# VectorE adds the epsilon of the roots, and six products take their remainder terms last

## Chip, cores and metric

The kernel runs on one core of one Trainium2 chip. The metric is device time in microseconds (us): the median of three runs.

## The reference

Two layers on a sequence of 256 positions with model width 1024, in float32. Layer 0 mixes with block-sparse attention (16 heads of 64; with one block of 256 it is plain causal attention), layer 1 with differential attention (8 heads, two softmaxes each, and a root mean square norm per head). Each mixer is followed by a squared-ReLU MLP of width 4096. Both are modulated by a conditioning vector and closed with a layer norm:

```python
for i in range(DEPTH):
    shift1, scale1, gate1, shift2, scale2, gate2 = split(mod[i], 6)
    h = x * (1.0 + scale1) + shift1
    y = moba_attention(h, ...) if i % 2 == 0 else diff_attention(h, ...)
    x = layer_norm(DEEPNORM_ALPHA * x + (1.0 + gate1) * y, ln_g[i, 0], ln_b[i, 0])
    h = x * (1.0 + scale2) + shift2
    y = square(relu(h @ mlp_w_up[i])) @ mlp_w_down[i]
    x = layer_norm(DEEPNORM_ALPHA * x + (1.0 + gate2) * y, ln_g[i, 1], ln_b[i, 1])
```

`layer_norm` and the norm per head both need `rsqrt(variance + 1e-5)`.

## The kernel before

The 256 positions are two blocks of 128 (b = 0, 1). TensorE works on pairs of numbers: each operand is split into a rounded part (hi) and the remainder (lo). A product takes three terms per depth of 128: hi x hi, hi x lo of the weights, lo of the activations x hi (lines 165 to 169). Weights arrive by DMA on SP's queue into `raw`; ScalarE casts a piece of 128x1024 to `hi` (line 130), VectorE subtracts to get `lo` (line 131, "the split"). `hi` and `lo` have eight slots each; a piece covers two depths, a weight set of 512 columns has four pieces.

A string of steps, PROGRAM, gives the order in which work is traced. For layer 1 it begins `V00 Q00 T00 S0 V10 Q10 ...` (values, queries with keys, transposes, scores; first digit the block), the MLP begins `U00 U01 X00 U10 U11 X01 ... D00` (up, transpose, down), `B` and `C` close a sub-layer, and `f` fills in a row of the modulation's matrix-vector product (line 216, VectorE). Each engine runs its own queue in order. The queue's order is laid out by a planner when the program is built: by the order of tracing among what it then expects to be ready, with `tc.high_priority()` for some instructions (only the scores use it). So instructions of later steps can stand between two dependent ones.

A closing (`close`, `layer_norm`, `modulate`) runs per block, eight times: six inner ones and two at the end of the kernel. VectorE makes z from the product, the gate and the residual (lines 289, 292) and takes statistics (302, 303). `rsqrt_eps` has GpSimd add the epsilon (277) and raise to the power -0.5 (278). VectorE scales the first half of z (308), ScalarE the second (311). TensorE transposes z (320), ScalarE modulates it (324) and casts it to the rounded operand `hT` (327), VectorE takes the remainder (328). Then the products of the next step can begin: V (layer 1) or U. The attention of layer 1 calls `rsqrt_eps` once for each of its eight pairs of heads and block, between ScalarE's squares (465) and VectorE's scaling (468). In the last closing VectorE subtracts the mean beside GpSimd's root (598) and then scales (601).

Of the kernel before, what the change touches and what calls it, by code (L numbers as in the profile page):

```python
# [19 lines left out]
ALU = mybir.AluOpType  # L20
# [12 lines left out]
EPS = 1e-5  # L33
# [39 lines left out]
def tile_trunk(ctx: ExitStack, tc: tile.TileContext, x, c, moba_w_in, moba_w_out, diff_w_in, diff_w_out,  # L73
               lam_q1, lam_k1, lam_q2, lam_k2, subln_g, ada_wt, ada_b, ln_g, ln_b, w_up, w_down, cst, out):
    nc = tc.nc
    vec, act, pe, pool_e, sp = nc.vector, nc.scalar, nc.tensor, nc.gpsimd, nc.sync
# [10 lines left out]
    def psum(tag):  # L87
        return psp.tile([P, 512], F32, tag=tag, name=tag, bufs=NB[tag])
# [48 lines left out]
    def load_cols(w, segs):  # L137

        ops = []
        for r in range(2):  # L140
            raw = raw_tile()
            r3 = raw.rearrange("p (k n) -> p k n", n=512)
            o = 0
            for c0, n in segs:
                sp.dma_start(out=r3[:, :, o:o + n],
                             in_=w[r * 512:(r + 1) * 512, c0:c0 + n].rearrange("(k p) n -> p k n", p=P))
                o += n
            for q in range(2):
                hi, lo = split_piece(raw[:, q * 1024:(q + 1) * 1024])
                for k in range(2):  # L150
                    ops.append((hi[:, k * 512:(k + 1) * 512], lo[:, k * 512:(k + 1) * 512]))
        return ops
# [12 lines left out]
    def mm3(dst, lhs, rhs, start, stop):  # L165
        (xh, xl), (wh, wl) = lhs, rhs
        pe.matmul(dst, lhsT=xh, rhs=wh, start=start, stop=False)  # L167
        pe.matmul(dst, lhsT=xh, rhs=wl, start=False, stop=False)  # L168
        pe.matmul(dst, lhsT=xl, rhs=wh, start=False, stop=stop)  # L169

    def dense(dst, lhs, rhs):
        n = len(lhs)
        for k in range(n):
            mm3(dst, lhs[k], rhs[k], k == 0, k == n - 1)

    def dense2(dsts, lhs, rows, start, stop):

# [80 lines left out]
    def halves(t, b):  # L258

        return t[:, :, b * P:(b + 1) * P], t[:, :, (2 + b) * P:(3 + b) * P]  # L260

    def as_ops(pairs):
        return [(h[:, k, :], l[:, k, :]) for h, l in pairs for k in range(4)]

    def block_ops(tiles, b):
        return as_ops([halves(t, b) for t in tiles])
# [7 lines left out]
        return t  # L274

    def rsqrt_eps(dst, src):
        pool_e.tensor_scalar(out=dst, in0=src, scalar1=EPS, scalar2=None, op0=ALU.add)
        pool_e.tensor_tensor(out=dst, in0=dst, in1=nhalf.to_broadcast(list(src.shape)), op=ALU.pow)

    def layer_norm(b, accs, gate, parts=None):  # L280
# [59 lines left out]
    def v_cols(g2):  # L340
        return [(2 * D + g2 * 512, 512)]
# [227 lines left out]
        queue_vector(*key)  # L569


    def unit(w, hT):
        ps = psum("mm")
        dense(ps, hT, w)
        return ps

    def out_proj(dsts, g2, b, rows):
# [36 lines left out]
    def step_load(st, key, loader):  # L614
        if key not in st:
            st[key] = loader()
        return st[key]

    def step_v(st, b, g2):
        l = st["l"]  # L620
        if l == 0 and g2 == 0:
            ps = kacc[b][0]
        else:
            w = step_load(st, ("wv", l, g2), lambda: load_cols(w_ins[l], v_cols(g2)))
            ps = unit(w, block_ops(st["x"], b))
        evict_v(b, g2, ps)

    def step_qk(st, b, g):
# [25 lines left out]
    def step_up(st, b, j):  # L654
        l = st["l"]
        w = step_load(st, ("wu", l, j), lambda: load_cols(w_up[l], [(j * 512, 512)]))
        ps = psum("mm")
        dense(ps, block_ops(st["x"], b), w)
        r = ap_.tile([P, 512], F32, tag="nat", name="nat", bufs=3)
        act.activation(out=r, in_=ps, func=AF.Relu)  # L660
        act.activation(out=r, in_=r, func=AF.Square)
        st["r", b, j] = r
# [75 lines left out]
    st = {"x": hT0}  # L738
# [48 lines left out]
```

## Time and profile before

| what | before |
|---|---|
| median of three runs | 643.16 us (641.18 to 646.57) |
| profiled execution | 644.11 us, of which the span of its instructions 640.7 |
| granted TensorE clock | 0.997 of full speed |
| busy: TensorE, VectorE, ScalarE, GpSimd | 609.0, 500.4, 377.6, 22.2 us |

The span runs from the first to the last instruction of the trace. Rows name the line, the engine (PE is TensorE, PEld its weight loads, DVE VectorE, ACT ScalarE, POOL GpSimd), the operation and its tiles, output before input.

### The profile page before, as it was taken

How to read it: one execution, taken by the hardware profiler on the slowest of the kernel's cores; microseconds unless marked ns; L12 is line 12 of the kernel's file. 1: busy time of each engine (PE TensorE's matmuls, PEld its weight loads, DVE VectorE, ACT ScalarE, POOL GpSimd, SP SyncE). 2: the span in 40 equal slices, each digit the busy share in tenths (PEclk: the TensorE clock that was granted, in tenths of full speed). 3: DMA queues.
4: the chain of work that ended last, by engine and by line, in shares of the span. 5: the costliest groups of instructions: out<-in, count | busy, mean ns of one | idle time of the engine just before them, and what ended most of it. 6: DMA issues, size and time to landing. Idle time of an engine off the chain costs nothing.

```text
span 640.7 us, 8768 instructions
## 1 busy us (share of the span) xinstructions
PE 609.0 (95%) x3140; PEld 499.6 (78%) x3140; DVE 500.4 (78%) x903; ACT 377.6 (59%) x699; POOL 22.2 (3%) x37
## 2 busy tenths in 40 slices
PE   4889999998999999999999999989999999999994
PEld 3667887886888888888877787767788888888883
DVE  5798998889978878888799989977984646465446
ACT  3448665657846545664477676765775556475530
POOL 0000000001000000000000010021100000000002
PEclk9999999999999999999999999999999999999998
DMA  8997998876689888989765967682663764746401
GB/s 292 406 322 279 313 325 286 288 250 227 215 309 343 308 313 330 326 294 338 268 231 188 337 229 263 232 289 68 208 218 109 259 225 143 255 133 213 182 0 66
DMA packets 65941, 158.23 MB, mean 247 GB/s; under 512 B 4041, under 2 KB 21098, under 8 KB 65898
## 3 DMA queue, kind: packets, MB, share of 16 engines
q1 hardware_dynamic: 65898, 157.68, 70.1%
q8 instruction: 24, 0.39, 0.2%
q14 instruction: 19, 0.16, 0.1%
HBM read 156.62 MB, written 1.05 MB: 246 GB/s over the span
## 4 chain that ended last, share of the span: by engine, by line
PE 64%; DVE 18%; DMA 6%; ACT 4%; issue 3%; POOL 2%; SPq 1%; DVEq 0%; POOLq 0%; ACTq 0%
PE ac L184 13%; PE sc L184 10%; PE mm L687 7%; PE tp L687 6%; DMA aw<-in_ada_w_dram 6%; DVE lo L131 5%; DVE aw L216 4%; PE mm L167 4%; PE mm L169 4%; PE mm L168 4%; PE mm L692 3%; PE tp L692 3%; ACT hi L130 2%; DVE z L292 1%; DVE z L289 1%
## 5 line engine op out<-in xcount | busy, mean ns | idle before, releaser
L131 DVE TENSOR_TENSOR lo<-raw,hi 128x1024 fp32r<-128x1024 f32 x196 | 232.0, 1197 | 44.1 <-ACT hi L130 40.4
L130 ACT CAST hi<-raw 128x1024 fp32r<-128x1024 f32 x196 | 201.3, 1034 | 62.5 <-PE sc L184 43.6
L216 DVE CUSTOM_DVE_ANT_0 aw<-aw,sbc,tabT 128x1024 f32<-128x1024 f32 x96 | 122.0, 1280 | 23.1 <-DMA aw<-in_ada_w_dram 22.7
L167 PE MATMUL mm<-hi,hT 128*128 128x512 f32 x224 | 90.6, 405 | 6.1 <-ACT hi L130 3.2
L169 PE MATMUL mm<-hi,hT 128*128 128x512 f32 x224 | 89.0, 398 | 0.0
L168 PE MATMUL mm<-lo,hT 128*128 128x512 f32 x224 | 88.6, 396 | 0.2 <-DVE lo L131 0.2
L687 PE MATMUL mm<-hT,hi 128*128 128x512 f32 x192 | 60.4, 396 | 0.0
L687 PE MATMUL tp<-hT,hi 128*128 128x512 f32 x192 | 60.3, 395 | 0.0
L167 PEld LDWEIGHTS mm<-hi,hT 128*128 128x128 f32 x224 | 42.3, 189 | 16.1 <-ACT hi L130 3.8
L184 PE MATMUL ac<-hi,sTh 128*128 128x512 f32 x160 | 51.2, 397 | 0.0
L184 PE MATMUL ac<-lo,sTh 128*128 128x512 f32 x160 | 50.8, 394 | 0.0
L184 PE MATMUL ac<-hi,sTl 128*128 128x512 f32 x160 | 50.4, 392 | 0.0
L169 PEld LDWEIGHTS mm<-hi,hT 128*128 128x128 f32 x224 | 42.3, 189 | 9.1 <-DVE hT L328 0.4
L168 PEld LDWEIGHTS mm<-lo,hT 128*128 128x128 f32 x224 | 42.3, 189 | 8.6 <-DVE lo L131 0.3
L184 PE MATMUL sc<-hi,sTh 128*128 128x512 f32 x144 | 45.3, 392 | 0.0
L184 PE MATMUL sc<-lo,sTh 128*128 128x512 f32 x144 | 45.1, 391 | 0.0
L184 PE MATMUL sc<-hi,sTl 128*128 128x512 f32 x144 | 44.6, 390 | 0.0
L692 PEld LDWEIGHTS tp<-hT,lo 128*128 128x128 f32 x192 | 34.4, 188 | 7.5
L692 PEld LDWEIGHTS mm<-hT,lo 128*128 128x128 f32 x192 | 34.4, 188 | 7.3
L697 ACT COPY nat<-mm 128x256 f32<-128x256 f32 x24 | 7.8, 376 | 52.4 <-PE mm L687 52.4
L692 PE MATMUL tp<-hT,lo 128*128 128x256 f32 x192 | 36.0, 279 | 0.0
L692 PE MATMUL mm<-hT,lo 128*128 128x256 f32 x192 | 35.9, 279 | 0.0
(153 smaller groups left out, 899.4 us busy)
## 6 DMA issues: line engine op xcount, KB each, us to landing
aw<-in_ada_w_dram SPq DMA_DIRECT2D x96, 512.0 KB, 5.5
raw<-in_mlp_w_up_dram SPq DMA_DIRECT2D x32, 1024.0 KB, 5.9
raw<-in_mlp_w_down_dram SPq DMA_DIRECT2D x32, 1024.0 KB, 5.1
raw<-in_diff_w_in_dram SPq DMA_DIRECT2D x16, 512.0 KB, 5.1
raw<-in_moba_w_in_dram SPq DMA_DIRECT2D x24, 256.0 KB, 5.5
raw<-in_moba_w_in_dram SPq DMA_DIRECT2D x8, 512.0 KB, 4.8
raw<-in_moba_w_out_dram SPq DMA_DIRECT2D x4, 1024.0 KB, 8.4
raw<-in_diff_w_in_dram SPq DMA_DIRECT2D x4, 1024.0 KB, 5.7
```

Source lines behind the costliest of these rows:

```text
L130: act.copy(out=hi[:, :n], in_=raw_ap)
L131: vec.tensor_tensor(out=lo[:, :n], in0=raw_ap, in1=hi[:, :n], op=ALU.subtract)
L167: pe.matmul(dst, lhsT=xh, rhs=wh, start=start, stop=False)
L168: pe.matmul(dst, lhsT=xh, rhs=wl, start=False, stop=False)
L169: pe.matmul(dst, lhsT=xl, rhs=wh, start=False, stop=stop)
L184: pe.matmul(dsts[h], lhsT=a, rhs=w[:, h * 512:(h + 1) * 512], start=start and k == 0 and i == 0, stop=stop and k == n - 1 and i == 2)
L216: vec.tensor_tensor_reduce(out=aw, in0=aw, in1=sbc, scale=1.0, scalar=adab_cols(l, v)[:, j:j + 1], op0=ALU.mult, op1=ALU.add, accum_out=dst)
L289: vec.tensor_tensor(out=z[:, c_], in0=accs[c_.start // 512][:, a0:a0 + c_.stop - c_.start], in1=gate[:, c_], op=ALU.mult)
L292: vec.scalar_tensor_tensor(out=z[:, c_], in0=xt[b][:, c_], scalar=ALPHA, in1=z[:, c_], op0=ALU.mult, op1=ALU.add)
L687: pe.matmul(ps, lhsT=w[k][0][:, c_], rhs=x3[k], start=first, stop=last)
L692: pe.matmul(ps[:, 0:S], lhsT=w[k][1][:, c_], rhs=x3[k][:, 0:S], start=False, stop=False)
L697: act.copy(out=r[:, i * S:(i + 1) * S], in_=ps[:, S:2 * S])
```

## The change

VectorE adds the epsilon instead of GpSimd; the power stays on GpSimd. A product marked `late` runs its two terms with the rounded activations over all eight depths first, and then the eight terms with the remainder of the activations. Marked are V00 and V10 of layer 1 (in layer 0 the products with g2 = 0 are made elsewhere) and U00, U10 of both layers. Neither edit raises the priority of an instruction.

```diff
-    def dense(dst, lhs, rhs):
+    def dense(dst, lhs, rhs, late=False):
+
         n = len(lhs)
+        if not late:
+            for k in range(n):
+                mm3(dst, lhs[k], rhs[k], k == 0, k == n - 1)
+            return
         for k in range(n):
-            mm3(dst, lhs[k], rhs[k], k == 0, k == n - 1)
+            for i in range(2):
+                pe.matmul(dst, lhsT=lhs[k][0], rhs=rhs[k][i], start=k == 0 and i == 0, stop=False)
+        for k in range(n):
+            pe.matmul(dst, lhsT=lhs[k][1], rhs=rhs[k][0], start=False, stop=k == n - 1)
...
     def rsqrt_eps(dst, src):
-        pool_e.tensor_scalar(out=dst, in0=src, scalar1=EPS, scalar2=None, op0=ALU.add)
+        vec.tensor_scalar(out=dst, in0=src, scalar1=EPS, scalar2=None, op0=ALU.add)
         pool_e.tensor_tensor(out=dst, in0=dst, in1=nhalf.to_broadcast(list(src.shape)), op=ALU.pow)
...
-    def unit(w, hT):
+    def unit(w, hT, late=False):
         ps = psum("mm")
-        dense(ps, hT, w)
+        dense(ps, hT, w, late)
         return ps
...
-            ps = unit(w, block_ops(st["x"], b))
+            ps = unit(w, block_ops(st["x"], b), late=g2 == 0)
         evict_v(b, g2, ps)
...
-        dense(ps, block_ops(st["x"], b), w)
+        dense(ps, block_ops(st["x"], b), w, late=j == 0)
```

## Rows read from the trace of the kernel before

**Rows 1.** Busy time by stretch (from:to, length, then busy us per engine, clock, DMA).
```profile
135.00:175.00 40.00, 37.45 (x177) 29.97 (x176) 38.06 (x52) 30.32 (x48) 3.30 (x4) 1.00 0.63 215
175.00:318.00 143.00, 143.00 (x728) 121.47 (x726) 116.48 (x162) 78.25 (x113) 0.00 (x0) 1.00 0.89 316
318.00:350.00 32.00, 31.06 (x152) 24.68 (x151) 30.34 (x45) 23.57 (x40) 3.15 (x4) 1.00 0.60 199
350.00:437.00 87.00, 83.40 (x468) 65.54 (x469) 76.91 (x218) 59.15 (x163) 7.96 (x14) 1.00 0.75 266
437.00:476.00 39.00, 38.09 (x181) 30.63 (x180) 34.12 (x47) 29.67 (x51) 4.25 (x6) 1.00 0.44 140
...
620.00:640.70 20.70, 11.83 (x57) 9.59 (x55) 14.18 (x26) 1.07 (x2) 3.26 (x4) 0.90 0.13 51
sum 640.70, PE 608.99 PEld 499.60 DVE 500.36 ACT 377.60 POOL 22.21; mean PE 76.12 PEld 62.45 DVE 62.55 ACT 47.20 POOL 2.78
```

**Rows 2.** The chain that ended last, one of its pieces (start, us, what).
```profile
190.74 5.45 PE sc L184 x24
```

**Rows 3.** Waits: who waited for whom (us in total, times, longest).
```profile
DVE on L468 <- POOL ss L278: 6.4, 7, 1.6
PE tp L320 <- DVE nm L310: 1.8, 3, 1.0
PE tp L320 <- DVE z L308: 1.5, 3, 0.5
PE mm L167 <- ACT hT L327: 1.1, 1, 1.1
PEld mm L169 <- DVE hT L328: 0.4, 1, 0.4
```

**Rows 4.** Line 277 alone (ns min/median/max, first and last start, shapes).
```profile
L277 POOL TENSOR_SCALAR rs<-bna x8: 705/1044/1087, 142.8 to 634.5; 128x1 f32<-128x1 f32 x8
L277 POOL TENSOR_SCALAR ss<-ss x8: 217/266/1192, 368.0 to 437.6; 128x2 f32<-128x2 f32 x8
```

**Rows 5.** Timeline of the sixth closing, VectorE and GpSimd (start, us, what, idle before).
```profile
455.46 0.68 DVE L302 BATCH_NORM_STATS2 bns<-z 128x6 f32<-128x512 f32 x1
...
456.05 1.21 DVE L131 TENSOR_TENSOR lo<-raw,hi 128x1024 fp32r<-128x1024 f32 x1
...
457.17 0.20 DVE L303 BATCH_NORM_AGGREGATE bna<-bns 128x2 f32<-128x12 f32 x1
457.29 1.17 DVE L131 TENSOR_TENSOR lo<-raw,hi 128x1024 fp32r<-128x1024 f32 x1
...
457.47 1.08 POOL L277 TENSOR_SCALAR rs<-bna 128x1 f32<-128x1 f32 x1 [11.32 <-DVE bna L303]
...
458.63 0.58 POOL L278 TENSOR_TENSOR rs<-rs,nhalf 128x1 f32<-128x1 f32 x1
...
459.25 0.55 DVE L308 TENSOR_SCALAR z<-z,bna,rs 128x512 f32<-128x512 f32 x1 [0.78 <-POOL rs L278]
...
459.78 1.22 DVE L131 TENSOR_TENSOR lo<-raw,hi 128x1024 fp32r<-128x1024 f32 x1
```

**Rows 6.** Groups of instructions: a VectorE operation on 128x1 (busy us, mean ns).
```profile
L440 DVE TENSOR_TENSOR sums<-sums,nlam 128x1 f32<-128x1 f32 x16 | 2.5, 155 | 0.1
```

**Rows 7.** Timeline behind the second closing: a cast released by U10, and D00's first matmuls.
```profile
163.28 1.05 ACT L130 CAST hi<-raw 128x1024 fp32r<-128x1024 f32 x1 [0.23 <-PE mm L169]
...
173.42 0.70 PE L184 MATMUL ac<-hi,sTh 128*128 128x512 f32 x2
```

**Rows 8.** Timeline of the last closing, VectorE and GpSimd.
```profile
634.41 1.41 DVE L598 SCALAR_TENSOR_TENSOR z<-z,bna,bc 128x512 f32<-128x512 f32 x2
634.53 0.70 POOL L277 TENSOR_SCALAR rs<-bna 128x1 f32<-128x1 f32 x1 [7.41 <-DVE bna L303]
635.32 0.92 POOL L278 TENSOR_TENSOR rs<-rs,nhalf 128x1 f32<-128x1 f32 x1
636.28 1.41 DVE L601 SCALAR_TENSOR_TENSOR z<-z,rs,bc 128x512 f32<-128x512 f32 x2 [0.46 <-POOL rs L278]
```

## What the change will do to the time

> **What bounds the kernel now.** I read first the table of busy time by stretch [rows 1]. TensorE is busy 608.99 of 640.70 us, so 31.7 us are idle in all. From 175 to 318 us it has no idle time at all: there the products set the time, and nothing in this change removes a product. The time can only come from, or go to, the stretches with idle time. Three of them (135 to 175, 318 to 350, 437 to 476) hold the six inner closings, with 2.55 + 0.94 + 0.91 = 4.40 us idle. The attention of the second layer (350 to 437) has 3.60, the tail from 620 on 8.87. The rest of the idle time lies in the start, where neither edit acts on the path (the first layer's attention has no root and its first products are not touched).
>
> Next, the chain that ended last gives the price of a product: 24 matmuls of 512 columns in 5.45 us, 0.227 us each [rows 2]. Then the waits [rows 3]: at the six inner closings TensorE waits 1.8 + 1.5 us in all before the transposes of z (line 320), and once 1.1 us for the rounded operand (hT, line 327). For a remainder (hT, line 328) it waits once, 0.4 us, and that on the weight load only. VectorE waits 6.4 us in seven places for the root of the attention (line 468).
>
> **The add on VectorE, six inner closings.** What is removed is one GpSimd instruction, line 277. It shows 1.04 us at the median in the closings, but 0.217 at the least and 0.266 at the median in the attention [rows 4]. The timeline of one closing says why [rows 5]: the statistics end at 457.17 + 0.20 = 457.37; the weight split of line 131 runs on VectorE from 457.29 to 458.46; the add on GpSimd starts at 457.47 and ends at 458.55, 0.09 after the split. The six inner closings repeat this, with an end 0.07 to 0.09 us after the split's. So of the 1.04 us some 0.8 is waiting until the split is over, not adding. The Trainium skill, "SBUF — State Buffer", section "Who interferes with whom", has a rule for it: GpSimd and VectorE share one pair of ports, and a VectorE instruction with two inputs in SBUF blocks a GpSimd one that reads SBUF until it is over. The ends 0.09 us after the split agree with it.
>
> What is added is one VectorE instruction on 128x1 elements; the nearest row takes 0.155 us (line 440, two inputs; the add has one) [rows 6]. Where it lands in VectorE's queue decides, and the trace of before cannot show that. Three places, worked out on the closing of [rows 5]:
>
> - *Behind the split.* The planner put a split between two dependent steps already: the last statistics end at 456.14, the split runs from 456.05, and only then comes line 303. If it does the same between line 303 and the add, the add runs from 458.46 to 458.61, the power (line 278, 0.58 us) from about 458.70 instead of 458.63, and line 308 starts at 459.32 instead of 459.25. That is +0.07 us: nothing.
> - *Ahead of the split.* The add ends at 457.53, the power is sent at about 457.63, but the split now runs until 458.70. If the power waits for it as the add did and needs another 0.42 us, as the power of the tail did after its neighbour (635.82 to 636.24, [rows 8]), line 308 starts at 459.16: -0.09 us. If nothing runs beside the power, it ends at 458.21 and line 308 starts at 458.25: -1.0 us.
> - *Behind one split and with a second beside the power.* The add ends at 458.61, the second split at 459.75, the power 0.42 later, line 308 at 460.21: +0.96 us.
>
> I take the first, at 0 us: it is what the planner did one step earlier in the same chain, and it turns the wait for the split on GpSimd into the same wait on VectorE. The bounds for six closings: the gain can't exceed the 4.40 us that TensorE idles there; the loss is at most 6 x 0.96 = 5.8 us, since TensorE already waits for each of the six z.
>
> By the skill's rule alone (the power, blocked whole, starts over at the end of the split) the second place would give 458.70 + 0.58 = 459.28 and so no gain either. That speaks against the change wherever a split runs beside the power.
>
> **The add in the attention of the second layer.** Eight adds of 0.266 us at the median (1.19 at most) give way to 0.155 us: some 0.1 us for most sites, 1.0 for the slowest. Line 468 already waits for the root in seven of eight. Against it, an add that the planner queues behind a split comes up to 1.17 us late. What follows line 468 is a transpose that the program places a step or more later, so most of either is covered by TensorE's other work; without that cover the eight are worth between -3.6 us (all the idle time of that stretch) and +8 x 1.17 = +9.4. I take -0.2.
>
> **The terms with remainders last.** Six products (V00, V10 of layer 1; U00, U10 of both layers) keep their 24 matmuls, and the eight with the lower part of the activations move behind the sixteen others. No instruction, DMA or weight load is added. The remainder is then needed 16 x 0.227 = 3.6 us after the first matmul. What can be gained is the wait for it: 0.4 us on a weight load, once, which cost the product behind it about 0.1 us. The 1.1 us wait is for the rounded part and stays: that one is needed first in either order. The planner also mixes the terms today by what it expects to be ready. So -0.1.
>
> The other side is the slots. A rounded weight piece covers two of the eight depths and has eight slots; today the first of four is free after 6 of the 24 matmuls, then after 18: 12 x 0.227 = 2.7 us later for the product of block 1, which is the last user. ScalarE's casts follow such releases. The cast at 163.28 waited for one of them, and D00, the next product but one, starts at 173.42 [rows 7]. Cast (1.05) and split (1.17) moved by 2.7 us end at 163.28 + 2.7 + 1.05 + 1.17 = 168.2, or 5.2 us before that product. I take 0. If this cover were gone, three late products of block 1 cost up to 3 x 2.7 = 8.2 us.
>
> **The tail.** The last root has nothing behind it. GpSimd's add starts at 634.53, its power ends at 636.24, line 601 waits 0.46 us and starts at 636.28 [rows 8]. With the add on VectorE, line 598 moves back by 0.15 and its two halves end at 635.97; the power is sent at about 634.68, waits for the first half and is done before the second ends. Line 601 then starts right after line 598, at about 636.05: -0.2 us. Bounds: -0.31, and +0.15 if the power has to wait for the second half.
>
> **Sum.** 0 - 0.2 - 0.1 + 0 - 0.2 = -0.5 us. The profiled execution took 644.11 us (span 640.7 and 3.4 around it), 0.95 above the median of 643.16; it becomes 643.6, and the median 642.7.
>
> **The rivals.**
>
> - *The add comes first and the power runs alone* (the change does what it says). For it: 0.22 us of GpSimd work and two hops do become 0.155 and one. Against it: in the six inner closings a split stands behind line 303, so splits are at hand. It gives up to -4.4 at the closings and -0.5 elsewhere: about 638.5 us.
> - *A second split beside the power*, with line 308 late by 0.96 us. For it: a split stands at once behind the scaled z again (459.78, [rows 5]), so it could have been ready. Against it: today VectorE idles 0.78 us there and the planner put none in. If all six fall so, 642.7 + 5.8 = 648.5 us; it is slower than before from the first closing on where TensorE has no product left to put in.
> - *The slots.* The late release holds up casts and splits of the next weights: at most 642.7 + 8.2 = 650.9 us. It decides once the 5.2 us of cover are used up by work that VectorE or ScalarE has to do first.
> - The planner lays every queue out anew, so small shifts elsewhere come on top of any case; I allow 1.5 us either way.
>
> **How the numbers follow.** Chances: the forecast 0.52 (its own range 641 to 644.5), the add first 0.18 (638.5 to 641), a second split 0.20 (643.5 to 648.5), the slots 0.10 (644 to 651). Leaving out the far end of the slots, half of the second split's upper third and the extreme of the first rival, the range is 639 to 648. One per cent, about what a measurement of this kernel can tell from no change, is 6.4 us: below 636.7 no case reaches without luck elsewhere, 0.07; above 649.6 lies part of the slots' case and the worst of the second split with shifts on top, 0.09; so 0.84 within.
>
> **What the profile after would show.** The add as VectorE work at 0.15 us, sixteen times, and GpSimd with the power alone. In the inner closings: what stands between line 303, the add and line 308, and whether line 308 starts 1.9 us after the end of line 303 as today (forecast), about 0.9 (add first, alone) or 2.8 (second split). The power should end 0.4 us behind a split that runs beside it; one of 0.58 us inside such a split would show that they don't block each other. The wait for line 328 should be gone. TensorE's idle time in the three closing stretches should stay near 4.4 us. The forecast is wrong if that sum moves by more than 2 us, or if waits for casts or splits of weights (line 130 or 131) appear in front of products behind V10 or U10.

## The result and the profile after

| | median, range, executions | before beside it | ratio, 95% interval |
|---|---|---|---|
| changed kernel | 647.20 us (643.89 to 653.14, 15) | 642.81 us (641.18 to 648.46, 15) | 1.0059 (1.0031 to 1.0087) |

The change makes the kernel slower by 0.6%, 4.4 us, and the interval of the ratio (worked out over all runs of both kernels, not from the two medians) stays above 1. That lies inside the range and inside the 1% that I called "same", but on the other side of the forecast of 642.7 us. The profiled execution of the changed kernel took 648.67 us, its span 645.9.

Lines behind the edited product moved by 8: the add is line 285 and stands on VectorE, the power line 286, the statistics 311, the scaled z 316, the transposes 328, the rounded part of hT 335 and its remainder 336. The rounded terms of a late product are line 180, the remainder terms 182. Casts and splits of weights are still lines 130 and 131.

The new page's totals of the engines (busy us, share of the span, instructions):

```profile
PE 611.6 (95%) x3140; PEld 500.6 (78%) x3140; DVE 500.4 (77%) x919; ACT 376.2 (58%) x699; POOL 18.0 (3%) x21
```

TensorE runs the same 3140 matmuls as before, yet is busy 2.6 us longer than the 609.0 us of [rows 1]. Busy time by stretch, columns as in [rows 1]:

```profile
135.00:175.00 40.00, 37.70 (x172) 30.55 (x171) 36.92 (x54) 28.82 (x47) 2.86 (x2) 0.96 0.61 207
175.00:318.00 143.00, 143.00 (x725) 121.41 (x724) 114.92 (x158) 79.07 (x112) 0.00 (x0) 1.00 0.90 313
318.00:350.00 32.00, 29.88 (x138) 23.33 (x136) 30.59 (x49) 19.75 (x35) 2.79 (x2) 1.00 0.65 219
350.00:437.00 87.00, 81.08 (x460) 63.57 (x460) 76.36 (x220) 60.94 (x164) 6.59 (x7) 1.00 0.75 257
437.00:476.00 39.00, 37.52 (x178) 29.30 (x177) 29.14 (x48) 23.86 (x45) 3.63 (x3) 1.00 0.33 116
```

Three things differ from [rows 1]. The clock column of the first stretch fell from 1.00 to 0.96. TensorE's idle time in the three closing stretches is 2.30 + 2.12 + 1.48 = 5.90 us instead of 4.40. In the attention of layer 2 it is 5.92 instead of 3.60.

These windows are fixed, while the closings move by up to 6 us from one trace to the other. Between like events, here from the statistics of closing 3 to those of closing 5, the same table reads (first before, then changed):

```profile
323.65:444.10 120.45, 115.91 (x625) 91.19 (x624) 107.12 (x263) 82.73 (x204) 12.04 (x20) 1.00 0.66 231
325.68:449.25 123.57, 114.79 (x616) 89.50 (x615) 107.81 (x275) 80.58 (x203) 10.07 (x10) 1.00 0.66 225
```

TensorE idles 8.78 us there instead of 4.54. From closing 1 to 3 it idles 2.30 instead of 2.55 us, from closing 5 to the last statistics 3.02 instead of 3.19. So the idle time that the change added lies between closings 3 and 5, across the attention of layer 2.

The add and the power, each by its line (ns min/median/max, first and last start, shapes):

```profile
L285 DVE TENSOR_SCALAR rs<-bna x8: 143/149/154, 142.5 to 640.1; 128x1 f32<-128x1 f32 x8
L286 POOL TENSOR_TENSOR rs<-rs,nhalf x8: 922/1394/1471, 142.8 to 640.4; 128x1 f32<-128x1 f32 x8
L286 POOL TENSOR_TENSOR ss<-ss,nhalf x8: 688/690/1603, 376.1 to 443.1; 128x2 f32<-128x2 f32 x8
```

The add costs 0.15 us, as estimated. But the power, 0.58 us in [rows 5], now takes 1.39 us at the median. The wait for a neighbour did not vanish; it moved from the add to the power. The sixth closing shows it (timeline, VectorE and GpSimd; compare [rows 5]):

```profile
463.18 0.20 DVE L311 BATCH_NORM_AGGREGATE bna<-bns 128x2 f32<-128x12 f32 x1
463.30 1.17 DVE L131 TENSOR_TENSOR lo<-raw,hi 128x1024 fp32r<-128x1024 f32 x1
464.39 0.14 DVE L285 TENSOR_SCALAR rs<-bna 128x1 f32<-128x1 f32 x1
464.45 1.21 DVE L340 TENSOR_TENSOR z<-z,bc 128x1024 f32<-128x1024 f32 x1
464.61 1.47 POOL L286 TENSOR_TENSOR rs<-rs,nhalf 128x1 f32<-128x1 f32 x1 [12.46 <-DVE rs L285]
466.12 0.55 DVE L316 TENSOR_SCALAR z<-z,bna,rs 128x512 f32<-128x512 f32 x1 [0.45 <-POOL rs L286]
```

Between the add and the scaled z the planner put one more VectorE instruction of two inputs: here the second half of block 0's residual (line 340), in closing 4 its first half (line 339), in closings 1, 2, 3 and 5 a second weight split. The power ends 0.42 us behind it (464.45 + 1.21 = 465.66, against 466.08). The scaled z starts 2.73 to 2.81 us after the end of the statistics in all six closings; before it was 1.85 to 1.88. That is the rival "a second split beside the power", at 0.87 to 0.95 us a closing.

This is the delay of z, and not yet one of TensorE. What TensorE waited for at the inner closings (compare the rows for lines 320 and 167 in [rows 3]):

```profile
PE tp L328 <- DVE nm L318: 2.3, 2, 1.9
PE mm L180 <- ACT hT L335: 1.8, 2, 1.6
PE tp L328 <- DVE z L316: 0.4, 2, 0.3
PE tp L328 <- ACT z L319: 0.3, 1, 0.3
```

That is 4.8 us in all against 1.8 + 1.5 + 1.1 = 4.4 before. The queues around the closings are new as well: block 1's statistics end 7.7 us behind block 0's at closing 2, where it was 10.8 before.

Behind the first closing the same delay starts something that the prediction did not have. TensorE's timeline there, then its clock in windows of 2 us (last three columns: clock, DMA share, GB/s):

```profile
144.88 0.63 PE L328 MATMUL tp<-cs,z 128*128 128x128 f32 x4 [0.46 <-DVE nm L318]
145.77 0.66 PE L328 MATMUL tp<-cs,z 128*128 128x128 f32 x4 [0.26 <-ACT z L319]
148.01 0.50 PE L180 MATMUL mm<-hi,hT 128*128 128x512 f32 x1 [1.58 <-ACT hT L335]
...
148.81 0.53 PE L180 MATMUL mm<-lo,hT 128*128 128x512 f32 x1
...
152.13 0.48 PE L180 MATMUL mm<-hi,hT 128*128 128x512 f32 x1
```

```profile
148.00:150.00 2.00, 1.99 (x7) 1.57 (x8) 2.00 (x4) 2.00 (x5) 0.00 (x0) 0.73 0.05 10
150.00:152.00 2.00, 2.00 (x6) 1.61 (x5) 2.00 (x5) 1.41 (x2) 1.47 (x1) 0.50 0.17 27
152.00:154.00 2.00, 2.00 (x9) 1.58 (x9) 2.00 (x4) 0.81 (x1) 0.00 (x0) 0.92 0.97 395
```

Before, products of the step ahead stood between the two halves of the transposes and behind them:

```profile
145.65 0.71 PE L184 MATMUL sc<-lo,sTh 128*128 128x512 f32 x2
146.20 0.61 PE L320 MATMUL tp<-cs,z 128*128 128x128 f32 x4
146.57 0.70 PE L184 MATMUL sc<-hi,sTl 128*128 128x512 f32 x2
```

With z late, TensorE had used these up, and waited 1.58 us for hT (1.1 in [rows 3]). Then the granted clock fell to 0.50 of full speed, the 1.2 GHz level. From 148.81 to 152.13 eight matmuls start in 3.32 us, where eight at the 0.227 us of [rows 2] take 1.82: 1.5 us lost, all of it in "busy" time.

The tail did gain (timeline; compare [rows 8]):

```profile
639.81 0.26 DVE L311 BATCH_NORM_AGGREGATE bna<-bns 128x2 f32<-128x24 f32 x1
640.11 0.15 DVE L285 TENSOR_SCALAR rs<-bna 128x1 f32<-128x1 f32 x1
640.18 1.40 DVE L606 SCALAR_TENSOR_TENSOR z<-z,bna,bc 128x512 f32<-128x512 f32 x2
640.41 0.92 POOL L286 TENSOR_TENSOR rs<-rs,nhalf 128x1 f32<-128x1 f32 x1 [8.20 <-DVE rs L285]
641.50 1.41 DVE L609 SCALAR_TENSOR_TENSOR z<-z,rs,bc 128x512 f32<-128x512 f32 x2
```

The wait of 0.46 us in [rows 8] is gone. From the last statistics to the end of the span it is 645.9 - 639.81 = 6.1 us instead of 640.7 - 634.1 = 6.6.

In the attention of layer 2 stands one long wait. A cast of weights, ScalarE's, and what VectorE and TensorE waited for behind it (timelines):

```profile
349.80 2.01 ACT L130 CAST hi<-raw 128x1024 fp32r<-128x1024 f32 x2 [2.67 <-PE mm L182]
...
361.32 1.05 ACT L130 CAST hi<-raw 128x1024 fp32r<-128x1024 f32 x1 [2.69 <-DMA raw<-in_diff_w_in_dram]
...
362.70 0.35 DVE L450 SCALAR_TENSOR_TENSOR p<-p,sums 128x128 f32<-128x128 f32 x1 [2.65 <-ACT p L449]
...
364.80 0.63 PE L374 MATMUL tp<-cs,nat 128*128 128x128 f32 x4 [2.57 <-DVE nat L367]
```

The casts behind V10 begin at 349.80 instead of 344.71 us and are released by a remainder term (line 182), the last in V10's new order. One cast 11.5 us later then waits for its transfer; ScalarE's next instruction (line 449) and VectorE behind it come late, and TensorE idles 2.57 us. TensorE also waits 2.1 us in two places for line 476, VectorE's scaling in the attention: two of the eight powers there take 1.60 and 1.53 us beside a weight split, where all eight took 0.71 before.

### The profile page after: what moved, and what is told of

It reads as the page before. It is cut to its first block, busy times and chain, and to the rows that moved or that the text cites. A ratio compares the mean times of both kernels' runs of the same rounds, so it can differ in the third digit from the quotient of the medians.

```text
span 645.9 us, 8752 instructions
## 1 busy us (share of the span) xinstructions
PE 611.6 (95%) x3140; PEld 500.6 (78%) x3140; DVE 500.4 (77%) x919; ACT 376.2 (58%) x699; POOL 18.0 (3%) x21
## 4 chain that ended last, share of the span: by engine, by line
PE 60%; DVE 18%; DMA 10%; issue 4%; ACT 4%; POOL 2%; SPq 1%; DVEq 0%; ACTq 0%; POOLq 0%
PE ac L192 13%; PE sc L192 9%; DMA aw<-in_ada_w_dram 8%; PE mm L695 6%; DVE lo L131 6%; PE tp L695 5%; DVE aw L224 4%; PE mm L167 3%; PE mm L169 3%; PE mm L168 3%; PE mm L700 3%; PE tp L700 3%; PE mm L180 2%; PE sc L425 1%; ACT hi L130 1%
## 5 line engine op out<-in xcount | busy, mean ns | idle before, releaser
L167 PE MATMUL mm<-hi,hT 128*128 128x512 f32 x176 | 71.6, 408 | 5.5 <-ACT hi L130 3.8
L169 PE MATMUL mm<-hi,hT 128*128 128x512 f32 x176 | 70.2, 399 | 0.0
L168 PE MATMUL mm<-lo,hT 128*128 128x512 f32 x176 | 70.0, 399 | 0.2 <-DVE lo L131 0.2
L167 PEld LDWEIGHTS mm<-hi,hT 128*128 128x128 f32 x176 | 33.4, 190 | 13.6 <-ACT hi L130 4.5
L168 PEld LDWEIGHTS mm<-lo,hT 128*128 128x128 f32 x176 | 33.2, 189 | 7.0 <-DVE lo L131 0.4
L169 PEld LDWEIGHTS mm<-hi,hT 128*128 128x128 f32 x176 | 33.2, 189 | 6.7
```

## The experiments

Theories: *the place* (VectorE's second instruction beside the power costs 0.9 us a closing, and the clock 1.5 us once), *the slots* (late products free the weight pieces late), and as rival *the plan as a whole* (any new order of the queues costs as much). All ratios are to runs of the kernel before on the same chip; like the first, they are worked out over all runs.

### Each edit alone

The add alone, from the changed kernel:

```diff
-            ps = unit(w, block_ops(st["x"], b), late=g2 == 0)
+            ps = unit(w, block_ops(st["x"], b), late=False)
...
-        dense(ps, block_ops(st["x"], b), w, late=j == 0)
+        dense(ps, block_ops(st["x"], b), w, late=False)
```

Late alone (for "late, block 0 alone" the two conditions also get `and b == 0`):

```diff
-        vec.tensor_scalar(out=dst, in0=src, scalar1=EPS, scalar2=None, op0=ALU.add)
+        pool_e.tensor_scalar(out=dst, in0=src, scalar1=EPS, scalar2=None, op0=ALU.add)
```

> Only the add moves to VectorE; no product is marked late. Theory 'second split' (a VectorE instruction beside the power holds it up): the power takes 1.4 us instead of 0.58 wherever a split or a residual stands beside it, the scaled z starts 2.6 to 2.8 us behind the end of the statistics instead of 1.9 in all six inner closings, and the median is 2 to 3 us above before. Theory 'slots' (the late products free the weights' slots late): at most +1 us, and the casts behind V10 come as early as before (345 to 350 us). Theory 'new plan' (only the two edits together make a bad order): within 1 us of before.

> Only the six products are marked late; the add stays on GpSimd. Theory 'slots': the first cast behind V10 comes about 4 to 5 us later than before, a cast then waits 2 us or more for the weights' transfer near 361 us, and the median is 2 to 3 us above before. Theory 'second split': within 0.7 us of before, since the closings keep one split beside GpSimd. Theory 'new plan': within 1 us.

> Late only for block 0 (V00, U00), the add on GpSimd. Block 0 is not the last user of a weight set, so slots come free as in before. Theory 'slots': what the late products lost is back, the median is within 0.7 us of before and the casts behind V10 follow every second depth as in before (0.3 us waits). If the loss of the late products lay in the order of the terms itself, this kernel keeps half of it: +1 us or more. Theory 'second split' says nothing else than for the late products alone: within 0.7 us.

> The kernel before once more, for one look: how far the same program moves between two profiled executions. All theories expect the same order, 640 to 646 us, and the six distances from the statistics to the scaled z at 1.9 us; places where it moves by 1 us or more by itself (waits on transfers) are no evidence for any theory.

| | median | ratio |
|---|---|---|
| add alone | 646.79 us | 1.0068 (1.0050 to 1.0086) |
| late alone | 643.78 us | 1.0011 (0.9988 to 1.0033) |
| late, block 0 alone | 642.62 us | 1.0005 (0.9986 to 1.0024) |
| before, once more (one execution) | 640.72 us | |

The add alone costs about what the whole change costs (1.0068 and 1.0059); its six closings and its clock behind the first are those of the changed kernel. The late products alone can't be told from before. The theory of the slots had expected 2 to 3 us from them: the casts behind V10 did come 3.5 us later, counted from the statistics of closing 3, but none waited for a transfer near 361 us. The kernel before, profiled again, has every inner closing 1.2 to 2.1 us earlier than in the first profile, so single clock times of two traces don't compare. Stretches between like events do: the table gives us from the statistics of closing 1 to those of closing 3, from there to closing 5, and from there to the last statistics.

| profiled kernel | 1 to 3 | 3 to 5 | 5 to last | sum |
|---|---|---|---|---|
| before; before again | 181.1; 181.7 | 120.5; 119.6 | 190.0; 190.0 | 491.6; 491.3 |
| changed | 184.5 | 123.6 | 190.6 | 498.6 |
| add alone | 183.7 | 121.6 | 191.7 | 497.0 |
| late alone | 183.8 | 121.0 | 190.0 | 494.8 |
| late, block 0 alone | 181.2 | 120.3 | 190.0 | 491.5 |
| add in the closings alone | 183.2 | 119.7 | 190.6 | 493.6 |
| add in the attention alone | 181.6 | 120.1 | 190.0 | 491.7 |
| one split, held (first try) | 186.1 | 118.9 | 190.2 | 495.3 |
| one split, held; again | 180.9; 180.9 | 119.0; 118.9 | 190.2; 190.2 | 490.1; 490.0 |
| the same, add on GpSimd | 181.2 | 119.6 | 190.8 | 491.5 |
| no split, held (first try) | 187.2 | 120.8 | 194.4 | 502.4 |
| no split, held | 183.7 | 119.2 | 190.0 | 492.9 |
| one split, held, all six late | 181.8 | 123.2 | 190.1 | 495.2 |
| one split, held, V late | 180.9 | 122.4 | 190.2 | 493.5 |
| one split, held, U late | 181.9 | 119.0 | 190.2 | 491.0 |
| one split, held, block 0 late | 181.8 | 119.1 | 190.2 | 491.0 |

In the profile of late alone TensorE waited 3.5 us for z in closing 3 and the clock fell to 0.50 there, which no other profile shows at that closing; VectorE's wait for a modulation row's transfer ahead of that closing (4.24 us) stands in before too (3.75).

A stretch doesn't hold the same products in every kernel. From closing 1 to 3 the two profiles of before have 893 and 898 matmuls, the changed kernel 903, late alone 902, add alone 895, add in the closings 896; what a stretch has more the next one mostly has less. Nine matmuls are 2 us, so single stretches of these kernels compare only to that, and the sums better.

### The add in the closings or in the attention

```diff
-    def rsqrt_eps(dst, src):
-        vec.tensor_scalar(out=dst, in0=src, scalar1=EPS, scalar2=None, op0=ALU.add)
+    def rsqrt_eps(dst, src, eng):
+        eng.tensor_scalar(out=dst, in0=src, scalar1=EPS, scalar2=None, op0=ALU.add)
...
```

> The add of the roots stands on VectorE in the six inner closings and the closing of the tail only; in the attention it is back on GpSimd, and all products keep the order of before. Theory of the second split: the inner closings carry the loss, so this kernel is as slow as the one with all adds on VectorE, 1.004 to 1.008 of before (646 to 648 us), with a second weight split beside the power of GpSimd, the power at 1.3 to 1.5 us and the scaled z 2.8 us behind the end of the statistics. Rival, the attention: the adds of its eight roots are what costs; then this kernel is within 0.2% of before. Rival, the plan as a whole: any new order of the queues costs about as much; then it is slower, but so are the others, the one with the add in the attention alone too.

> The add stands on VectorE only in the eight roots of the attention of the second layer; the closings are as before, with the add on GpSimd, and so are the products. Theory of the second split: within 0.2% of before (642 to 644 us), with the scaled z 1.9 us behind the end of the statistics. Rival, the attention: the eight powers that wait for a neighbour on VectorE there (1.35 to 1.67 us in three of eight) cost the loss; then 1.004 to 1.008. Rival, the plan as a whole: 1.003 or more, although no closing is longer.

In the closings alone: 644.38 us, 1.0020 (0.9992 to 1.0048). In the attention alone: 643.23 us, 0.9996 (0.9972 to 1.0020). So the attention by itself costs nothing, and "the plan as a whole" falls for it: that plan is new too. The closings have z 2.72 to 2.80 us behind the statistics and the same fall of the clock; the stretch from 1 to 3 is 1.5 to 2.1 us longer than before, which the clock alone (1.5) comes near to, and the sum is about 2 us longer. So six late z by themselves did not cost the 1.004 to 1.008 that was expected, and the timing is inconclusive: it bears anything from no loss to 0.5%. The add everywhere takes 1.9 us more between closings 3 and 5 and 1.1 us more behind them than the add in the closings alone, though the attention's adds alone lose nothing there. That part needs both and stays open. TensorE's waits for line 476 don't settle it: they are 1.8 us with the attention's adds alone, where no time was lost, 2.2 with the add alone and 0.3 with the add in the closings alone.

### VectorE's queue held by hand

To put the add where the prediction had it, splits, rows of the modulation and residuals were tied behind the closing's last VectorE instruction; a table says which one goes behind which closing. No wait is added, only VectorE's order is fixed; the planner lays the rest out around it.

```diff
+    def behind(ins, closing):
+        if closing is not None and closing < len(nms):
+            tc.add_manual_dep(ins.ins, nms[closing].ins.name,
...
-        vec.tensor_tensor(out=lo[:, :n], in0=raw_ap, in1=hi[:, :n], op=ALU.subtract)
+        sub = vec.tensor_tensor(out=lo[:, :n], in0=raw_ap, in1=hi[:, :n], op=ALU.subtract)
+        behind(sub, SPLITS.get(len(count)))
```

In these kernels the add is line 300, the power 301, the statistics 326, the scaled z 331, the transposes 344; casts and splits are lines 141 and 142, rows of the modulation 237. In the first try rows of the modulation still fell into the even closings.

> All adds on VectorE, products as before. The weight splits are held by hand so that in the inner closings one of them stands between the statistics and the add and none beside the power: the place that the prediction took. In the first, third and fifth closing nothing else comes between; in the second, fourth and sixth a row of the next layer's modulation falls in beside the power. Theory of the second split: in closings 1, 3 and 5 the power takes 0.57 us and the scaled z starts 1.8 to 2.0 us behind the end of the statistics, as before; in 2, 4 and 6 still 1.2 to 1.6 us of power; in all about half of the loss is gone, 1.002 to 1.005 of before, and TensorE's clock does not fall behind the first closing. Rival, the plan as a whole: the closings are short and the time stays at 1.006 to 1.008. Rival, the add itself (VectorE's add or its hand-over to GpSimd is slow wherever it stands): the scaled z stays 2.8 us behind the statistics.

> All adds on VectorE, products as before. The weight splits are held by hand so that in closings 1, 3 and 5 the add follows the statistics and nothing stands on VectorE beside the power; in closings 2 and 6 rows of the next layer's modulation still fall in before the add and beside the power, in 4 one before the add. Theory of the second split: in closings 1, 3 and 5 the power takes 0.57 us and the scaled z starts about 0.95 us behind the end of the statistics, 0.9 less than before; if TensorE's wait at these closings shrinks by as much, up to 0.9 us each are gained in them, 0.998 to 1.003 of before in all. Rival, GpSimd does not care what stands beside it (the longer power comes from the kind of its input): the power still takes 1.4 us with nothing beside it. Rival, the plan as a whole: 1.006 or more with short closings.

One split: 645.06 us, 1.0020 (1.0000 to 1.0041). No split: 651.76 us, 1.0126 (1.0097 to 1.0155). The totals say little, the closings say much. Closings 1 and 2 of the first kernel, timeline:

```profile
143.14 0.55 POOL L301 TENSOR_TENSOR rs<-rs,nhalf 128x1 f32<-128x1 f32 x1 [142.30 <-DVE rs L300]
...
153.96 1.27 DVE L237 CUSTOM_DVE_ANT_0 aw<-aw,sbc,tabT 128x1024 f32<-128x1024 f32 x1
154.12 1.53 POOL L301 TENSOR_TENSOR rs<-rs,nhalf 128x1 f32<-128x1 f32 x1 [10.43 <-DVE rs L300]
```

The same power in one run: 0.55 us with nothing beside it, 1.53 us beside a row. In closings 1, 3 and 5 the scaled z comes 1.82 to 1.97 us after the statistics with one split, 0.86 to 0.93 with none; in the even ones 2.79 to 2.87 and 1.95 to 3.60. That settles what lengthens the power. The totals are spoilt by closing 2: block 0's residual stood ahead of block 1's statistics and two rows between these and the scaled z, TensorE waited 3.5 and 6.1 us for z, and its clock fell to 0.50 at that wait in both (in the second kernel once more behind closing 6). My expectation had named the rows, but not what they cost: with no split it was 0.998 to 1.003.

### The place of the prediction, in all six closings

Now the rows and residuals are tied as well, so that nothing stands beside the power in any inner closing. Beside it the same kernel with the add on GpSimd (line 300 alone differs), and one without a split.

> All adds on VectorE, products as before, and in all six inner closings VectorE's queue is held by hand: one weight split between the statistics and the add and nothing beside the power (closings 1, 3 to 6), or no split at all (closing 2). Rows of the modulation and the residual products are held behind the closings. Theory of the place: the power takes 0.55 us in all six, the scaled z starts 2.0 us behind the end of the statistics (0.95 in closing 2), no wait of 2 us and no fall of TensorE's clock stands behind closings 1 and 2, and the loss is gone: 0.998 to 1.002 of before. Rival, the plan as a whole: short closings, but 1.004 or more, since the queues of ScalarE, TensorE and the transfers are laid out anew. Rival, the attention: the adds there keep about 1 us, 1.002.

> The queue held by hand as in the kernel before it in this list, the add on GpSimd as in the kernel before the change: the two differ in the engine of one line alone. Theory of the place: the add takes 1.0 us beside a split and 0.22 us in closing 2, where none stands beside it, the power 0.57 us, and the time is within 0.2% of the kernel with the add on VectorE in the same place, for the engine of the add alone is worth 0.1 us a closing. Rival, VectorE's add is slow by itself: this one is faster by 0.4% or more. Rival, holding the queue costs: both are slower than before by as much.

> All adds on VectorE, products as before; VectorE's queue held so that the add follows the statistics directly in all six inner closings and nothing stands beside the power. Theory of the place: power 0.55 us, scaled z 0.95 us behind the statistics in all six, 0.9 less than before, and no new wait from modulation rows: 0.994 to 0.999 of before, a gain of up to 0.9 us a closing as far as TensorE's waits there follow. Rival, the rest of the queue: what is held back (six splits and the residuals) comes late for the products behind the closing, and TensorE waits for splits of weights instead: 1.000 or more.

| VectorE's queue held | median | ratio |
|---|---|---|
| one split, add on VectorE | 640.07 us | 0.9952 (0.9930 to 0.9974) |
| one split, add on GpSimd | 641.65 us | 0.9992 (0.9965 to 1.0018) |
| no split, add on VectorE | 642.67 us | 0.9989 (0.9966 to 1.0012) |

The power of the first, by its line, and TensorE's clock behind its first closing (windows of 2 us):

```profile
L301 POOL TENSOR_TENSOR rs<-rs,nhalf x8: 547/553/922, 143.6 to 632.7; 128x1 f32<-128x1 f32 x8
```

```profile
148.00:150.00 2.00, 1.68 (x6) 1.10 (x7) 2.00 (x5) 1.68 (x4) 0.00 (x0) 1.00 0.36 128
150.00:152.00 2.00, 2.00 (x11) 1.60 (x10) 1.40 (x4) 1.81 (x2) 0.45 (x1) 1.00 0.00 0
```

With the add in the forecast's place z comes 1.83 to 1.97 us behind the statistics (0.86 in closing 2), the clock stays at 1.00, and the loss of the add is not only gone: the kernel is 0.5% faster than before, more than the 0.998 to 1.002 expected. No kernel here is clearly faster. Holding the queue is not by itself the gain: with the add on GpSimd it gives 0.9992. The engine of line 300 alone, which serves all sixteen roots, is worth 2.3 us (0.8 to 3.8) by the means of the twelve runs of each, some 0.4% where 0.2% at most was expected. The stretches of the table are 0.3, 0.6 and 0.6 us shorter than with the add on GpSimd, but two profiles of before differ by as much in a stretch, and the profiled run with the add on GpSimd was its slowest (647.7 us). VectorE's add is not slow; its place was.

With no split z comes 0.85 to 0.94 us behind the statistics everywhere, a microsecond earlier than before, and nothing is gained: 0.9989, against the 0.994 to 0.999 expected, and 2.5 us more than with one split by the means. Closings 3 to 6 give the same stretches as with one split (119.2 and 190.0). At the second closing TensorE, out of other products, waited 2.4 us for z, where it waits 0.17 us with one split, and the clock fell once more to 0.50 (timeline):

```profile
154.15 0.66 PE L344 MATMUL tp<-cs,z 128*128 128x128 f32 x4 [2.41 <-DVE z L331]
```

### The late products, with the closings held

> Both edits of the change as they are (all adds on VectorE, six products with the remainder terms last), with VectorE's queue at the inner closings held by hand as above. Theory of the place: 0.998 to 1.002 of before; the change loses nothing once its add stands where the prediction put it. Rival, the slots: the late products hold the casts of the next weights up and cost 1 to 3 us in the attention of layer 2 on top of the kernel without them, 1.002 to 1.005, with a cast that waits for a transfer near 361 us.

Both edits, held: 643.90 us, 0.9995 (0.9970 to 1.0019), 3.8 us above the same without late products by the medians and 2.9 (1.7 to 4.1) by the means. So the theory's "0.998 to 1.002" came true for a wrong reason: the late products cost what the good place of the add had gained. The stretch from 3 to 5 is 123.2 us instead of 119.0, with a cast at 360.37 that waits 3.02 us for its transfer. Three more kernels ask which product it is.

"V late" puts `late=False` at U, "U late" puts it at V, "block 0 late" is this:

```diff
-            ps = unit(w, block_ops(st["x"], b), late=g2 == 0)
+            ps = unit(w, block_ops(st["x"], b), late=g2 == 0 and b == 0)
...
-        dense(ps, block_ops(st["x"], b), w, late=j == 0)
+        dense(ps, block_ops(st["x"], b), w, late=j == 0 and b == 0)
```

> The kernel with all adds on VectorE, products as before, and the queue of VectorE held by hand at the six inner closings, run again as the base of the three kernels beside it: 0.993 to 0.998 of before, if the gain seen once is real. Rival: the gain was of one chip; then 0.998 to 1.002.

> As the base, with the remainder terms last in the products of block 0 alone (V00 of layer 1, U00 of both layers); block 1, the last user of the weight pieces, keeps the order of before. Theory of the slots: the pieces come free as early as in the base, no cast waits for a transfer near 360 us, and the time is within 0.2% of the base. Rival, the late order itself costs (remainders that are ready are left standing): half of the 0.4% between the base and the kernel with all six products late stays, and more if it sits in block 0.

> As the base, with the remainder terms last in V00 and V10 of layer 1 alone. Theory of the slots, at V10: the casts behind V10 start some 3 to 4 us later, their raw pieces come free later, the transfers for the projections of the attention start later and a cast waits 3 us for one near 360 us; 0.3 to 0.6% over the base. Rival, the slots at U10: within 0.2% of the base.

> As the base, with the remainder terms last in U00 and U10 of both layers alone. Theory of the slots, at V10: the cover of 5.2 us between U10's casts and D00 holds and the time is within 0.2% of the base, with casts as in the base near 360 us. Rival, the slots at U10: 0.3 to 0.6% over the base, with waits for casts or splits behind U10.

| closings held, one split | median | ratio |
|---|---|---|
| none late (base) | 640.57 us | 0.9945 (0.9922 to 0.9967) |
| V00, U00 late (block 0) | 640.17 us | 0.9956 (0.9934 to 0.9979) |
| U00, U10 late | 641.20 us | 0.9957 (0.9934 to 0.9980) |
| V00, V10 late | 642.36 us | 0.9981 (0.9957 to 1.0005) |

The gain of the base repeats on another chip. These four ran side by side there, so their means compare directly: V late is 2.2 us (1.2 to 3.2) above the base, U late 1.0 (0.1 to 1.9), block 0 late 0.5 (-0.5 to 1.5). For V late the stretch from 3 to 5 shows where: 122.4 us against 118.9 to 119.1 in the other three. ScalarE's casts behind V10, first the base, then V late (timelines):

```profile
345.01 1.06 ACT L141 CAST hi<-raw 128x1024 fp32r<-128x1024 f32 x1 [0.36 <-PE mm L182]
```

```profile
347.12 2.94 ACT L141 CAST hi<-raw 128x1024 fp32r<-128x1024 f32 x3
...
357.94 2.00 ACT L141 CAST hi<-raw 128x1024 fp32r<-128x1024 f32 x2 [1.99 <-DMA raw<-in_diff_w_in_dram]
```

From the statistics of closing 3 the first cast comes 347.12 - 322.31 = 24.8 us later, in the base 345.01 - 323.62 = 21.4: 3.4 us. From then on the casts run close together, but the next transfers of these weights are issued 1.6 to 2.9 us later than in the base, and one cast waits 1.99 us for its data. TensorE's longest wait in that stretch, 1.39 us for line 384 at 364.61, follows; a modulation row also stands on VectorE ahead of it, so the chain from the cast to that wait is not shown link by link. V10's late remainders are the cause of the longer stretch, and block 0's are not.

U00 late has a price of its own, at closing 2. The stretch from 1 to 3 is 181.8 to 181.9 us in the three held kernels that have it and 180.9 in the three that don't. TensorE's transposes of block 1, first in the base, then with block 0 late (timelines):

```profile
153.37 0.66 PE L344 MATMUL tp<-cs,z 128*128 128x128 f32 x4 [0.21 <-DVE z L331]
```

```profile
154.80 0.66 PE L344 MATMUL tp<-cs,z 128*128 128x128 f32 x4 [1.23 <-DVE z L331]
```

Both stand 4.69 us behind the first matmul of U00 (148.68 and 150.11). In the base sixteen matmuls fill that time, five of them remainder terms; with U00 late there are fourteen, none of them a remainder term, and TensorE waits for z. That is the rival "remainders that are ready are left standing", at 0.9 us; it fits the 1.0 us of U late.

## Why the prediction was wrong, step by step

- **The add in the six closings, 0 us: wrong, and this is the step that decided.** "I take the first [place] ... it is what the planner did one step earlier in the same chain." The planner did that, and then put another VectorE instruction beside the power: the third place, at +0.96 us for z, and 0.87 to 0.95 measured. With all adds on VectorE the kernel is 0.68% slower on the planner's order and 0.5% faster when the forecast's place is held. That the rival's 648.5 us came near the 647.2 measured is luck in part: its 5.8 us carry every late z to TensorE in full, "since TensorE already waits for each of the six z". TensorE's waits at the closings were 4.8 us instead of 4.4, and the add in the closings alone lengthened the stretches by about 2 us, most of it at the lower clock. What turns these 2 us into the 5 to 6 of all adds needs the attention's adds too, and its cause stays open. What misled me was the argument "today VectorE idles 0.78 us there and the planner put none in". In the order of before the add was on GpSimd and the gap was what followed it; with the add in VectorE's own queue the planner filled the gap behind it. The experiments show the consequence, not why the planner chose so.
- **How the power behaves beside a neighbour: right.** It ends 0.41 to 0.42 us behind the neighbour's end, as I took from [rows 8], and takes 0.55 alone. By the Trainium skill, "SBUF — State Buffer", section "Who interferes with whom", a GpSimd instruction that reads SBUF is blocked while VectorE runs one with two inputs in SBUF. The traces agree as to the block; by a power that is blocked whole, 0.55 us should follow it, and 0.42 did.
- **TensorE's clock: missing.** No term had it, since in before it is 1.00 in all inner stretches [rows 1]. It took about 1.5 us of the stretch from 1 to 3. The sign that I named would have overlooked it: "TensorE's idle time ... should stay near 4.4 us" counts a matmul at half speed as busy, and it looked at the closings only. Over the whole span idle time grew by 2.6 us (31.7 to 34.3) and busy time by 2.6.
- **The slots: the mechanism was there, the cover was sized at the wrong product.** I worked out 5.2 us of cover between U10's casts and D00, and that held: with U late the casts behind U10 wait 0.53 us for a transfer, no more than the 1.31 of the base, and the 0.9 us of U late stand at closing 2. I did not work it out for V10, whose casts are followed by transfers for the next projections; those 3.4 us (2.7 in the prediction) ended in a wait for data, as the second sign had it. With the closings held V late costs 2.2 us and all six 2.9 by the means. Alone, on the plan of before, the late products cost 0.11%, which can't be told from nothing (interval -0.1 to +0.3%). In the changed kernel the stretch from 3 to 5 is 2.0 us longer than with the add alone, but the two medians stand against different runs of before (1.0059 and 1.0068), so that the late products' share of the 4.4 us was not measured there.
- **The add in the attention, -0.2 us: not contradicted** (0.9996), but the interval is 0.24% or 1.5 us either way, so it can't be told. VectorE's wait for the root went from the 6.4 us of [rows 3] to 5.7 us in seven, while two powers became longer by 0.8 to 0.9 us. Together with the closings it loses more, which is open.
- **Late terms, -0.1 us: the sign was wrong where it could be seen.** The wait for the remainder of hT [rows 3] is gone, as said, but with the closings held U00's late order cost 0.9 us at closing 2. The term had priced the wait for remainders and not the use of remainders that are ready as filling. On the plan of before (block 0 late alone) no such loss shows: 181.2 against 181.1 and 181.7.
- **The tail, -0.2 us: right in kind, 0.5 us in size.** Line 609 follows line 606 without a wait.
- **The gain of the first place was priced too low.** Where the add really stood there, the kernel gained 0.5%, some 3 us. The stretches show about 1.5 us of it and the tail 0.5. The closing 2 without a split in that kernel may be one cause; it has the same place with the add on GpSimd, and nothing was separated further.
- **The rival "the add comes first" was priced too high.** It was given up to 4.4 us at the closings, all of TensorE's idle time there. With z a microsecond earlier in all six, nothing was gained (0.9989). (4.4 and 0.5 from 643.16 would also be 638.3 and not 638.5.)

The largest single lesson for the sum: a range of +0.96 us a closing was on the table with its price, and I chose between places by an argument on the planner instead of leaving both at like odds. The second is that a delay of z was taken for a delay of TensorE, which depends on the products that stand ready at each closing.

## What to carry to other kernels

An instruction moved to the busiest queue takes the place that the planner gives it there, and the work behind it moves too: price the instruction that then stands beside the *next* step, not only the one moved. When a small GpSimd operation seems slow, see what VectorE does during it; here 0.55 us became 1.4 to 1.5. Changing the engine lost 0.7% with the neighbour beside the next step and gained 0.5% without it. A product that keeps its operands longer must be checked for cover at every place where it stands, down to the transfer that waits for the buffer. Terms that are ready early also fill waits, so moving them last can open one. And a check on TensorE must read busy time and clock together, since at half clock a lost microsecond looks like work.

## What the runs showed of the hardware that was not expected

- A wait of TensorE of 1.58 to 1.59 us for hT, with two shorter ones ahead of it (0.46 and 0.26 us in the changed kernel), was followed by the clock at 0.50 for about 3 us in the changed kernel, in the one with the add alone and in the one with the add in the closings. A wait of 1.35 to 1.36 us in the kernels held by hand with one split left it at 1.00, and so did 1.13 us in the kernel before. The rows don't tell what between them decides. With 1.58 us of waiting instead of 1.13 came 1.5 us of loss at the lower clock.
- GpSimd's power on 128x1 takes 0.55 us alone when VectorE hands it its input and 0.57 to 0.58 behind GpSimd's own add; its [128x2] form 0.69 and 0.71. GpSimd's add takes 0.22 us alone and 1.0 us beside a split. Neither is slow in itself.
- VectorE starts the scaled z 0.85 to 0.94 us after the statistics when nothing stands between them (add, hand-over, power, hand-over): the shortest that these kernels show for this step, and having it in all six closings gained nothing by itself.
